# A bank copy on VectorE in the state-space stage, full-partition masks and later scaling and turns in the delta rule

## The chip, the cores and the metric

The program runs on one core of a Trainium2 chip. Its engines work side by side, each through its own instruction queue in order: TensorE (PE in the profile, with its weight loads as PEld), VectorE (DVE), ScalarE (ACT), GpSimd (POOL) and the queue of SyncE (SP), which only starts DMA transfers here. The metric is the device time of one execution in microseconds (us). A profile of one execution gives a row for each instruction.

## The reference, cut to what matters

Three layers on 256 tokens of width 1024: sparse attention, a state-space mixer and a gated delta rule, each followed by a gated feed-forward network. The change touches the second and the third mixer:

```python
def ssd_mixer(h, w_in, conv_w, conv_b, dt_bias, a_log, d_skip, norm_w, w_out):
    proj = h @ w_in
    z = proj[..., :SSD_D_INNER]
    xbc = jax.nn.silu(causal_dwconv(proj[..., SSD_D_INNER:SSD_D_INNER + SSD_CONV_DIM], conv_w, conv_b))
    ...
    y = ssd_scan(x_ssm, dt, a, bm, cm) + d_skip[:, None] * x_ssm
    y = y.reshape(b, s, SSD_D_INNER) * jax.nn.silu(z)
    ...

def gated_delta_rule(q, k, v, a, b, a_log, dt_bias):       # 8 heads, chunks of 64 tokens
    q = l2norm(q) * GDN_DK ** -0.5
    k = l2norm(k)
    ...
    kk = jnp.einsum("bhnid,bhnjd->bhnij", kc, kc)
    lower = jnp.where(strict, bc[..., :, None] * kk * decay, 0.0)
    rhs = jnp.concatenate([vc * bc[..., None], kc * (bc * jnp.exp(G))[..., None]], axis=-1)
    sol = lax.linalg.triangular_solve(lower + jnp.eye(CHUNK), rhs, left_side=True, lower=True, unit_diagonal=True)
    u, w = sol[..., :GDN_DV], sol[..., GDN_DV:]
    p = jnp.einsum("bhnid,bhnjd->bhnij", qc, kc) * decay
    qg = qc * jnp.exp(G)[..., None]
    ...                                                     # a scan over the 4 chunks with u, w, qg, kg, p
```

## The kernel before, in words

Everything is float32. A product x·w of a projection is made as three matmuls of rounded parts: ScalarE writes the upper part of a weight (`whi`, line 361), VectorE or GpSimd the rest (`wlo`, line 362), and TensorE adds whi·xhi, whi·xlo and wlo·xhi (line 308). A projection is cut into slabs of 256 output columns. A slab takes 48 matmuls of 128x256 into one PSUM bank of the tag `u`, of which there are two; a function `evac` then takes the bank away. Other small products use two banks of the tag `b`.

TensorE's order is that of the program text. The other engines' queues are put in order at build time by priority and by when an instruction is expected to be ready; VectorE, ScalarE and GpSimd then work them off strictly in that order. Slabs wait in a queue of generators; `pace()` puts as much of them between two steps of a chain as the next number of a table says (`GF` for the delta rule), `need(x)` runs the queue until x is done.

**State-space stage (ssd).** 20 of its slabs end in `convsilu` (12: B, C and x, a causal convolution of four taps, then x·sigmoid(x)) or `gate` (8: z). Since the row scale is already in the activations here, `scaled` (line 744) hands out the PSUM bank itself: `conv` (line 754) has ScalarE write the last tap into `u` and the last but one into `tap`, VectorE adds two more taps (line 767) and GpSimd the `tap` tile (line 769); `silu2` (line 771) follows. VectorE's taps and ScalarE's reads go to the bank.

**Delta rule (gdn).** Slabs k, then q, then v0 to v3 (the values of heads 0-1, 2-3, 4-5, 6-7), then z. The chain on VectorE: `L` (lower) is made; lines 1616 to 1622 turn its 16x16 diagonal blocks to the partitions by masks (`xp`, 8 instructions on 32 partitions each), a 32x32 transpose and a sum `yf`; 15 steps of a product and a sum (lines 1628 and 1629) invert all the blocks; lines 1691 to 1700 spread the inverse out again into `T` (in the buffer `et`, which the decay matrix for `Pt` held before) and `U`, each by a memset and 8 masked copies on 32 partitions. `T` and `U` then grow to 64x64 by two levels of products on TensorE (`lev16`, `lev32`), ending in `ub`. `nw` is `rw` times `ub` (32 matmuls), and `scan` runs over the chunks with `ub`, `bv`, `nw`, `kg`, `qn` and `Pt`.

Beside that chain: `scale(qn, rG)` (line 1585 on) multiplies the queries by exp(G): four times a `pace()`, two broadcast matmuls `b<-rh,sel` and one VectorE multiplication by that bank (line 1594), before `T` and `U` are made. `k_turn` (kt0 to kt3) transposes keys on TensorE and fills `kg` and `rw`. `v_turn(s)` (b0 to b3) transposes the finished value slab s (a tile named `gpsq`) on TensorE, and VectorE multiplies it into `bv` (line 1670). `POOL_PG` (line 1688) sends all rests of weights to GpSimd from that point of the text on.

## Time and profile before

| | us |
|---|---|
| median of 3 runs | 1330.9 |
| lowest and highest of them | 1323.39 and 1338.49 |
| the profiled execution, device time | 1329.81 |
| span of its trace | 1328.0 |
| granted TensorE clock, mean over the span | 0.964 |
| TensorE / VectorE / ScalarE / GpSimd busy | 1246.6 / 896.1 / 715.9 / 226.9 |

Times in the trace count from the start of the span; the device time is 1.8 us longer than the span. The state-space stage lies at about 412 to 622 us, the delta rule at about 875 to 1092 us. The granted clock is 1.00 at TensorE's full speed (2.4 GHz) and 0.50 at half. An idle time in square brackets stands before the instruction that it delayed, with what ended it.

### The profile page before, as it was taken

Reading aid. Unit: us, or ns where it says so; the run is one execution under the profiler, and the core shown is the slowest. Engines: PE = TensorE matmul, PEld = TensorE weight load, DVE = VectorE, ACT = ScalarE, POOL = GpSimd, SP = SyncE. Lnnn points to the kernel's source line nnn. Section 1 sums busy time; section 2 is a strip of 40 time slices with the busy share of each in tenths; the row PEclk is TensorE's granted clock in tenths of the full one; section 3 lists DMA queues with packets and bytes.
Section 4 is the critical chain, followed back from the end, with each engine's and each line's share of the span. In section 5 each row is a group of like instructions: output and inputs, shape, how many; then the busy total and the mean of one; then the engine's idle time right before and its main releaser. Section 6 shows DMA issues by size and latency. Waiting matters only on the chain.

```text
span 1328.0 us, 22701 instructions
## 1 busy us (share of the span) xinstructions
PE 1246.6 (94%) x8874; PEld 1110.1 (84%) x8874; DVE 896.1 (67%) x1647; ACT 715.9 (54%) x1340; POOL 226.9 (17%) x149
## 2 busy tenths in 40 slices
...
GB/s 316 283 143 1 33 118 201 197 184 188 183 153 140 118 110 143 137 102 140 167 194 191 181 181 187 116 155 96 112 48 49 64 64 159 172 192 180 185 184 41
DMA packets 54108, 192.78 MB, mean 145 GB/s; under 512 B 6128, under 2 KB 6768, under 8 KB 53616
## 3 DMA queue, kind: packets, MB, share of 16 engines
...
## 4 chain that ended last, share of the span: by engine, by line
PE 49%; DVE 9%; issue 7%; ACT 3%; POOL 2%; DMA 0%; POOLq 0%; DVEq 0%; ACTq 0%
PE u L308 29%; PE acc L308 16%; PE b L308 3%; DVE u L767 2%; DVE wlo L362 1%; ACT whi L361 1%; PE b L313 1%; POOL wlo L362 1%; POOL x L1267 0%; POOL rs L457 0%; DVE et L1698 0%; DVE rs L459 0%; POOL l2r L1585 0%; DMA raw<-in_gdn_up_dram 0%; ACT u L762 0%
## 5 line engine op out<-in xcount | busy, mean ns | idle before, releaser
L361 ACT ACTIVATE whi<-raw 128x1024 fp32r<-128x1024 f32 (+1 forms) x342 | 356.1, 1048 | 255.9 <-PE u L308 122.2
L308 PE MATMUL u<-xhi,whi 128*128 128x256 f32 x1600 | 467.0, 292 | 12.3 <-DVE xp L1628 5.5
L362 DVE TENSOR_TENSOR wlo<-raw,whi 128x1024 fp32r<-128x1024 f32 (+1 forms) x283 | 351.3, 1247 | 183.8 <-ACT whi L361 181.7
L308 PE MATMUL u<-xlo,whi 128*128 128x256 f32 x1600 | 458.7, 287 | 0.0
L308 PE MATMUL u<-xhi,wlo 128*128 128x256 f32 x1600 | 458.6, 287 | 0.0
L308 PEld LDWEIGHTS u<-xhi,whi 128*128 128x128 f32 x1600 | 313.2, 196 | 20.5 <-issue 15.4
L308 PEld LDWEIGHTS u<-xlo,whi 128*128 128x128 f32 x1600 | 313.3, 196 | 2.3
L308 PEld LDWEIGHTS u<-xhi,wlo 128*128 128x128 f32 x1600 | 312.8, 196 | 0.0
L362 POOL TENSOR_TENSOR wlo<-raw,whi 128x1024 fp32r<-128x1024 f32 x59 | 145.4, 2474 | 207.5 <-ACT whi L361 205.0
L308 PE MATMUL acc<-whi,yhi 128*128 128x512 f32 x376 | 150.9, 401 | 0.1
L308 PE MATMUL acc<-whi,ylo 128*128 128x512 f32 x376 | 149.8, 398 | 0.6 <-DVE ylo L362 0.6
L308 PE MATMUL acc<-wlo,yhi 128*128 128x512 f32 x376 | 149.8, 398 | 0.0
L574 POOL TENSOR_TENSOR post<-post,mhalf 128x1 f32<-128x1 f32 x12 | 6.5, 544 | 533.3 <-DVE post L573 523.2
L308 PEld LDWEIGHTS acc<-whi,ylo 128*128 128x128 f32 x376 | 71.1, 189 | 18.4 <-DVE ylo L362 1.0
L308 PEld LDWEIGHTS acc<-whi,yhi 128*128 128x128 f32 x376 | 71.4, 190 | 15.6 <-ACT yhi L361 0.6
L308 PEld LDWEIGHTS acc<-wlo,yhi 128*128 128x128 f32 x376 | 70.9, 189 | 14.3
L361 ACT ACTIVATE yhi<-y 128x256 fp32r<-128x256 f32 x66 | 27.2, 412 | 41.7 <-DVE y L851 41.6
L767 DVE SCALAR_TENSOR_TENSOR u<-u,par,u 128x254 f32<-128x254 f32 (+2 forms) x100 | 46.0, 473 | 5.1 <-ACT u L760 2.4
L535 DVE SCALAR_TENSOR_TENSOR xlo<-b,par,xhi 128x128 fp32r<-128x128 f32 x80 | 24.7, 345 | 29.8 <-ACT xhi L534 29.4
L767 DVE SCALAR_TENSOR_TENSOR uv<-p,par,uv 128x255 f32<-128x255 f32 x80 | 42.6, 532 | 0.1
L308 PE MATMUL acc<-whi,xhi 128*128 128x256 f32 x160 | 34.2, 295 | 8.9 <-ACT xhi L534 8.9
L534 ACT ACTIVATE xhi<-b,par 128x128 fp32r<-128x128 f32 x80 | 25.5, 366 | 31.5 <-PE b L313 28.4
...
## 6 DMA issues: line engine op xcount, KB each, us to landing
...
```

Source lines behind the costliest of these rows:

```text
L308: self.nc.tensor.matmul(out, lhsT, rhs, start=start, stop=stop, skip_group_check=True)
L313: self.nc.tensor.transpose(out, in_, self.c("ident", n)[:, :n])
L361: self.nc.scalar.activation(hi, src, AF.Copy)
L362: return (lo_engine or self.nc.vector).tensor_sub(lo, src, hi.bitcast(F32))
L534: act = nc.scalar.activation(h, ps, AF.Copy, scale=self.pc(gain, k))
L535: return act, nc.vector.scalar_tensor_tensor(l, ps, self.pc(gain, k), h.bitcast(F32), op0=ALU.mult, op1=ALU.subtract)
L574: nc.gpsimd.tensor_tensor(r[:, one], ms[:, one], self.mhalf, op=ALU.pow)
L767: nc.vector.scalar_tensor_tensor(u[c][:, sh:], p[c][:, :S - sh], col(c, taps - 1 - sh), u[c][:, sh:], op0=ALU.mult, op1=ALU.add)
```

## The change

- **State-space stage.** `scaled` gets an argument `copy`; with it, and no row scale, VectorE copies the whole bank (128x512) into an SBUF tile `p` first, at high priority, and everything after it reads `p`. The tanh of `silu2` is written over `p` (or over `u` for the gates) and not into a tile of its own. GpSimd's addition of `tap` now stands before VectorE's two taps.
- **Delta rule, masks.** Four masks `block16` on all 128 partitions take the place of the pairs on 32 partitions: `xp` takes 4 instructions, of which two also add, and `T` and `U` 4 each without a memset. The sign moves into the sum `yf`.
- **Delta rule, order.** `scale(qn, rG)` comes after `ub`, its four places in `GF` are 0.0, and its old share (2.5 + 5.3) is one number 7.8 at the pace before `lev16`. b2 and b3 come after `nw`, straight before the scan.

```diff
@@ -38,7 +38,7 @@
 NF = (1.8, 4.3, 1.0, 1.7, 0.0, 25.4, 27.1, 36.4, 3.6, 0.6, 0.0, 1.7, 0.6, 0.0, 5.9, 0.0, 17.5, 0.6, 1.4, 1.6, 2.0, 0.0, 0.3, 0.9, 22.3, 0.7, 3.9, 10.1, 17.8, 8.3, 2.0, 7.7, 15.3)
 ATT = 1
 BF = (1.7, 1.8, 0.0, 1.5, 1.5, 9.5, 1.5, 1.3, 0.0, 1.5, 2.5, 9.5, 1.5, 2.5, 0.0, 1.5, 1.5, 0.0)
-GF = (5.0, 5.3, 5.2, 9.6, 0.0, 2.5, 0.0, 0.0, 5.3, 0.9, 2.0, 0.3, 0.0, 9.0, 15.1, 28.2, 3.0, 6.1, 0.0, 0.0, 1.3, 0.2, 2.3, 0.9, 1.8, 0.0, 0.5, 0.9, 0.0, 1.3, 0.7, 1.3, 0.0, 0.0, 0.0, 4.0, 2.1, 1.2, 1.3, 0.0, 1.0, 0.0, 0.3, 1.2, 0.0, 0.0, 2.1, 9.5, 0.0, 19.3)
+GF = (5.0, 5.3, 5.2, 9.6, 7.8, 0.9, 2.0, 0.3, 0.0, 9.0, 0.0, 0.0, 0.0, 0.0, 15.1, 28.2, 3.0, 6.1, 0.0, 0.0, 1.3, 0.2, 2.3, 0.9, 1.8, 0.0, 0.5, 0.9, 0.0, 1.3, 0.7, 1.3, 0.0, 0.0, 0.0, 4.0, 2.1, 1.2, 1.3, 0.0, 1.0, 0.0, 0.3, 1.2, 0.0, 0.0, 2.1, 9.5, 0.0, 19.3)
 W_POOL = ()
 W_AHEAD = 62
 LEAD_N = 108
@@ -86,8 +86,8 @@
     put("sel32", (np.arange(64)[:, None] % 32 == np.arange(32)[None, :]))
     put("sel8", (np.arange(40)[:, None] % 32 == np.arange(8)[None, :]))
     put("half", np.stack([i < 64, i >= 64], 1))
-    put("neg16", -np.stack([i % 32 < 16, i % 32 >= 16], 1).astype(np.float32))
-    put("pos16", np.stack([i % 32 < 16, i % 32 >= 16], 1))
+    block = np.stack([(i % 64 // 32 == b) & (i % 32 // 16 == a) for b in range(2) for a in range(2)], 1).astype(np.float32)
+    put("block16", block)
     q = np.stack([i, i + 128], 1)
     ok = (np.arange(16)[None, None, :] * 16 + 31) <= q[:, :, None]
     put("cmask", ok.reshape(P, 32))
@@ -741,8 +741,13 @@
             self.need("tail")
         return x
 
-    def scaled(self, pool, ps, rb, tag="p", bufs=2):
-
+    def scaled(self, pool, ps, rb, tag="p", bufs=2, copy=False):
+
+        if rb is None and copy:
+            p = pool.tile([P, 2, S], F32, tag=tag, name=self.nm(tag), bufs=bufs)
+            with self.tc.high_priority(offset=URGENT // 2):
+                self.nc.vector.tensor_copy(p, ps.rearrange("p (c s) -> p c s", c=2))
+            return p
         if rb is None:
             return ps.rearrange("p (c s) -> p c s", c=2)
         p = pool.tile([P, 2, S], F32, tag=tag, name=self.nm(tag), bufs=bufs)
@@ -762,11 +767,11 @@
                 nc.scalar.activation(u[c], p[c], AF.Identity, scale=col(c, taps - 1), bias=self.pc(bias, i[c]))
             if pool is not None:
                 nc.scalar.activation(pool[c], p[c], AF.Copy, scale=col(c, taps - 2))
+            if pool is not None:
+                nc.gpsimd.tensor_add(u[c][:, 1:], u[c][:, 1:], pool[c][:, :S - 1])
         for c in both:
             for sh in range(1 if pool is None else 2, taps):
                 nc.vector.scalar_tensor_tensor(u[c][:, sh:], p[c][:, :S - sh], col(c, taps - 1 - sh), u[c][:, sh:], op0=ALU.mult, op1=ALU.add)
-            if pool is not None:
-                nc.gpsimd.tensor_add(u[c][:, 1:], u[c][:, 1:], pool[c][:, :S - 1])
 
     def silu2(self, out, u, th):
 
@@ -1149,18 +1154,18 @@
             def convsilu(key, i, b=1):
 
                 def evac(ps, x):
-                    p = self.scaled(sp, ps, x.rb)
+                    p = self.scaled(sp, ps, x.rb, copy=True)
                     u, o = t("u", [P, 2, S], b=2), t(key if b == 1 else key[0], [P, 2, S], b=b)
                     pool = [self.np_.tile([P, S], F32, tag="sq", name=self.nm("tap"), bufs=3) for _ in range(2)]
                     self.conv((u[:, 0], u[:, 1]), (p[:, 0], p[:, 1]), "scw", (i, i + 1), 4, "scb", pool)
-                    self.silu2(o, u, t("th", [P, 2, S], b=2))
+                    self.silu2(o, u, p)
                     out[key] = o
                 return evac
 
             def gate(key):
                 def evac(ps, x):
-                    u, o = self.scaled(sp, ps, x.rb), t("z", [P, 2, S], b=4)
-                    self.silu2(o, u, t("th", [P, 2, S], b=2))
+                    u, o = self.scaled(sp, ps, x.rb, copy=True), t("z", [P, 2, S], b=4)
+                    self.silu2(o, u, t("u", [P, 2, S], b=2))
                     out[key] = o
                 return evac
 
@@ -1613,13 +1618,16 @@
 
             xp, yt = t("xp", [P, 16, 32]), t("yt", [P, 16, 32])
             yf, tb = (spare(tag, 1).rearrange("p (a b) -> p a b", a=16) for tag in ("psum", "sqs"))
-            quads = [(slice(32 * q, 32 * q + 32), 32 * (q % 2)) for q in range(4)]
-            for qs, o in quads:
-                for a in range(2):
-                    nc.vector.tensor_scalar(xp[qs, :, 16 * a:16 * a + 16].rearrange("p j u -> p u j"),
-                                            L[qs, :, o + 16 * a:o + 16 * a + 16], self.c("neg16")[qs, a:a + 1], None, op0=ALU.mult)
+            blocks = [(b, a, 32 * b + 16 * a) for b in range(2) for a in range(2)]
+            for b, a, o in blocks:
+                x16 = xp[:, :, 16 * a:16 * a + 16].rearrange("p j u -> p u j")
+                mask = self.c("block16")[:, 2 * b + a:2 * b + a + 1]
+                if b == 0:
+                    nc.vector.tensor_scalar(x16, L[:, :, o:o + 16], mask, None, op0=ALU.mult)
+                else:
+                    nc.vector.scalar_tensor_tensor(x16, L[:, :, o:o + 16], mask, x16, op0=ALU.mult, op1=ALU.add)
             nc.vector.transpose(yt.rearrange("p a b -> p (a b)"), xp.rearrange("p a b -> p (a b)"))
-            nc.vector.tensor_add(yf, yt[:, :, :16], yt[:, :, 16:])
+            nc.vector.scalar_tensor_tensor(yf, yt[:, :, :16], -1.0, yt[:, :, 16:], op0=ALU.mult, op1=ALU.subtract)
             pr = t("xp", [P, 16, 32]).rearrange("p a b -> p (a b)")
             nc.vector.memset(tb, 0.0)
             nc.vector.memset(tb.rearrange("p a b -> p (a b)")[:, ::17], 1.0)
@@ -1674,7 +1682,7 @@
             for s in range(4):
                 self.add(f"v{s}", v_slab(s))
                 self.add(f"kt{s}", k_turn(s // 2, s % 2))
-                if s:
+                if s in (1, 2):
                     self.add(f"b{s - 1}", v_turn(s - 1))
             self.pace()
             rq, rq2 = t("rq", [P, 2, 8]), t("rq2", [P, 2, 8])
@@ -1684,7 +1692,6 @@
             pq = each(lambda u, tt, h, c: (kn[:, h, cs(tt, c)], qn[:, h, cs(tt, c)]))
             for tt in range(2):
                 nc.vector.tensor_tensor(half(Pt, tt), pq[tt], half(et, tt), op=ALU.mult)
-            scale(qn, rG)
             self.pool_lo = POOL_PG
             with self.tc.high_priority(offset=URGENT // 2):
                 T, U = m("et"), m("U")
@@ -1692,12 +1699,9 @@
                     d2, z = t("xp", [P, 16, 2, 16]), t("yt", [P, 16, 32])
                     nc.vector.tensor_copy(d2, view[:, :, None, :].to_broadcast([P, 16, 2, 16]))
                     nc.vector.transpose(z.rearrange("p a b -> p (a b)"), d2.rearrange("p a b c -> p (a b c)"))
-                    nc.vector.memset(dst, 0.0)
-                    for qs, o in quads:
-                        for a in range(2):
-                            nc.vector.tensor_scalar(dst[qs, :, o + 16 * a:o + 16 * a + 16],
-                                                    z[qs, :, 16 * a:16 * a + 16].rearrange("p c u -> p u c"),
-                                                    self.c("pos16")[qs, a:a + 1], None, op0=ALU.mult)
+                    for b, a, o in blocks:
+                        nc.vector.tensor_scalar(dst[:, :, o:o + 16], z[:, :, 16 * a:16 * a + 16].rearrange("p c u -> p u c"),
+                                                self.c("block16")[:, 2 * b + a:2 * b + a + 1], None, op0=ALU.mult)
 
             def z_slab(s):
                 def evac(ps, x):
@@ -1705,8 +1709,6 @@
                         zs.append(t("rw", [P, 8, S]))
                     self.silu2(two(zs[0], s), self.scaled(gp, ps, x.rb), t("th", [P, 2, S]))
                 return evac
-
-            self.add("b3", v_turn(3))
 
 
             self.pace()
@@ -1745,6 +1747,8 @@
                     nc.vector.tensor_tensor(half(ub, tt)[rs(c), :, rs(c)], half(U, tt)[rs(c)], pu[tt][rs(c)], op=ALU.subtract)
             self.pace()
 
+            scale(qn, rG)
+
 
             self.need("kt3")
             nw = t("kn", [P, 16, P])
@@ -1759,6 +1763,8 @@
                                          AF.Copy, scale=-1.0)
             self.gains(gp, "el")
             z = [up(12 + s, x, z_slab(s)) for s in range(4)]
+            self.add("b2", v_turn(2))
+            self.add("b3", v_turn(3))
             self.add("z1", chain(z[0], z[1]))
             self.add("z3", between(attention(), chain(z[2], z[3]), 3) if LATE else chain(z[2], z[3]))
             self.need("b3")
```

TensorE, from the second level's last products to the scan. `b<-cst,kn` is kt3, `b<-cst,gpsq` are b2 and b3, `b<-ad,rw` is `nw`, `b<-rh,sel` is the scaling of the queries, `acc<-bv,ad` the start of the scan. Before:

```order
L308 MATMUL acc_11275<-el_10239,et_10971 64x64 x16
L313 MATMUL b_11328<-cst,kn_9636 128x128 x4
L313 MATMUL b_11338<-cst,gpsq_11044 128x128 x4
L313 MATMUL b_11345<-cst,gpsq_11324 128x128 x4
L308 MATMUL b_11353<-ad_11308,rw_9639 128x128 x4
L308 MATMUL b_11359<-ad_11308,rw_9639 128x128 x4
L308 MATMUL b_11365<-ad_11308,rw_9639 128x128 x4
L308 MATMUL b_11371<-ad_11308,rw_9639 128x128 x4
L308 MATMUL acc_11380<-bv_10676,ad_11308 128x128 x2
```

TensorE at the same place now:

```order
L308 MATMUL acc_11273<-el_10267,et_10918 64x64 x16
L313 MATMUL b_11326<-cst,kn_9664 128x128 x4
L308 MATMUL b_11336<-rh_10496,sel_81 128x256 x2
L308 MATMUL b_11340<-rh_10496,sel_81 128x256 x2
L308 MATMUL b_11344<-rh_10496,sel_81 128x256 x2
L308 MATMUL b_11348<-rh_10496,sel_81 128x256 x2
L308 MATMUL b_11353<-ad_11306,rw_9667 128x128 x4
L308 MATMUL b_11359<-ad_11306,rw_9667 128x128 x4
L308 MATMUL b_11365<-ad_11306,rw_9667 128x128 x4
L308 MATMUL b_11371<-ad_11306,rw_9667 128x128 x4
L313 MATMUL b_11379<-cst,gpsq_11042 128x128 x4
L313 MATMUL b_11386<-cst,gpsq_11322 128x128 x4
```

The transposes of the last two value slabs went behind `nw`, and the eight broadcasts of the queries' scale, which stood among the slabs v1 and v2, came in ahead of it.

VectorE, from the second half of `Pt` on (`u<-u,par,u` are taps of slab v1, `et` and `U` the masked copies). Before:

```order
L1686 TENSOR_TENSOR Pt_10857<-acc_10859,et_10240 128x512
L1594 TENSOR_TENSOR qn_9637<-qn_9637,b_10894 128x512
L1695 MEMSET et_10971 128x1024
L1639 TENSOR_TENSOR kg_9638<-b_10917,egl_10134 128x512
L1698 TENSOR_SCALAR et_10971<-yt_10974,cst 32x16x16 x8
L767 SCALAR_TENSOR_TENSOR u_10904<-u_10773,par,u_10904 128x255
L1694 STREAM_TRANSPOSE yt_10987<-xp_10986 128x512
L767 SCALAR_TENSOR_TENSOR u_10904<-u_10773,par,u_10904 128x254
L1698 TENSOR_SCALAR U_10972<-yt_10987,cst 32x16x16 x8
L767 SCALAR_TENSOR_TENSOR u_10904<-u_10773,par,u_10904 128x253
L767 SCALAR_TENSOR_TENSOR u_10904<-u_10773,par,u_10904 128x255
L1594 TENSOR_TENSOR qn_9637<-qn_9637,b_10959 128x512
```

VectorE at the same place now:

```order
L1694 TENSOR_TENSOR Pt_10881<-acc_10883,et_10268 128x512
L1703 TENSOR_SCALAR et_10918<-yt_10921,cst 128x16x16 x4
L1647 TENSOR_TENSOR kg_9666<-b_10955,egl_10162 128x512
L1701 STREAM_TRANSPOSE yt_10929<-xp_10928 128x512
L774 SCALAR_TENSOR_TENSOR u_10942<-u_10797,par,u_10942 128x255
L1703 TENSOR_SCALAR U_10919<-yt_10929,cst 128x16x16 x4
L774 SCALAR_TENSOR_TENSOR u_10942<-u_10797,par,u_10942 128x254
L1678 TENSOR_TENSOR bv_10700<-b_10965,bhr_10442 128x256
L774 SCALAR_TENSOR_TENSOR u_10942<-u_10797,par,u_10942 128x253
L774 SCALAR_TENSOR_TENSOR u_10942<-u_10797,par,u_10942 128x255
L1678 TENSOR_TENSOR bv_10700<-b_10965,bhr_10442 128x256
L774 SCALAR_TENSOR_TENSOR u_10942<-u_10797,par,u_10942 128x254
```

The multiplications of `qn` and the memset are gone from here, and 8 masked copies are 4.

VectorE in the state-space stage, about the two last slabs before its scan (`x` is the result of a slab, `ah` the row sums that the first broadcast there needs). Before:

```order
L362 TENSOR_TENSOR wlo_5273<-raw_5270,whi_5272 128x1024
L1198 TENSOR_TENSOR boff_5019<-acs_5018 128x32
L1199 TENSOR_SCALAR nacs_5020<-acs_5018 128x32
L774 SCALAR_TENSOR_TENSOR x_4949<-th_4962,u_4948 128x512
L767 SCALAR_TENSOR_TENSOR u_5036<-u_4977,par,u_5036 128x254
L1206 TENSOR_TENSOR ah_5056<-b_5053,ah_5056 32x256
L767 SCALAR_TENSOR_TENSOR u_5036<-u_4977,par,u_5036 128x253
```

VectorE at the same place now:

```order
L362 TENSOR_TENSOR wlo_5281<-raw_5278,whi_5280 128x1024
L1203 TENSOR_TENSOR boff_5024<-acs_5023 128x32
L1204 TENSOR_SCALAR nacs_5025<-acs_5023 128x32
L749 COPY p_5041<-u_4982 128x512
L779 SCALAR_TENSOR_TENSOR x_4955<-p_4952,u_4954 128x512
L1211 TENSOR_TENSOR ah_5062<-b_5059,ah_5062 32x256
L1221 SCALAR_TENSOR_TENSOR cb_5069<-b_5066,cst 128x128
L774 SCALAR_TENSOR_TENSOR u_5043<-p_5041,par,u_5043 128x254
```

The copy of the bank came in, the taps moved behind `ah`, and a tap's first operand is `p` in SBUF in place of the PSUM bank.

## Rows read from the trace of the kernel before

**Rows 1.** The page: busy time, share of the span and instructions of each engine.
```profile
PE 1246.6 (94%) x8874; PEld 1110.1 (84%) x8874; DVE 896.1 (67%) x1647; ACT 715.9 (54%) x1340; POOL 226.9 (17%) x149
```

**Rows 2.** Windows over both stages: length, busy us (instructions) by engine, granted clock.
```profile
412.00:622.00 210.00, 192.23 (x1324) 171.20 (x1325) 150.02 (x245) 113.70 (x230) 63.07 (x46) 0.94 0.38 126
875.00:1092.00 217.00, 183.59 (x1687) 173.67 (x1686) 124.90 (x270) 87.52 (x191) 58.41 (x25) 0.87 0.23 78
```

**Rows 3.** Waits of TensorE, 400 to 660 us: in total, times, longest.
```profile
PE b L308 <- DVE ah L1206: 2.8, 1, 2.8
...
PE u L308 <- DVE u L767: 1.6, 1, 1.6
```

**Rows 4.** Waits of TensorE, 860 to 1120 us.
```profile
PE b L308 <- DVE qn L1594: 9.1, 1, 9.1
PE b L313 <- DVE gpsq L774: 7.6, 1, 7.6
PE u L308 <- DVE xp L1628: 5.5, 1, 5.5
```

**Rows 5.** Timeline of TensorE in the delta rule: start, duration, instruction.
```profile
973.90 0.79 PE L308 MATMUL b<-rh,sel 40*128 40x256 f32 x2 [9.09 <-DVE qn L1594]
...
984.32 1.85 PE L308 MATMUL acc<-U,ad 64*64 64x64 f32 x56
...
999.98 0.66 PE L313 MATMUL b<-cst,kn 128*128 128x128 f32 x4
...
1008.65 1.11 PE L313 MATMUL b<-cst,gpsq 128*128 128x128 f32 x4 [7.58 <-DVE gpsq L774]
1009.56 4.85 PE L308 MATMUL b<-ad,rw 128*128 128x128 f32 x32
1014.24 1.95 PE L308 MATMUL acc<-bv,ad 128*128 128x128 f32 x16
```

**Rows 6.** Timeline of VectorE in the delta rule.
```profile
915.35 2.96 DVE L1619 TENSOR_SCALAR xp<-ad,cst 32x256 f32<-32x256 f32 x8
...
959.59 1.28 DVE L1686 TENSOR_TENSOR Pt<-acc,et 128x512 f32<-128x512 f32 x2
...
961.62 0.91 DVE L1695 MEMSET et<- 128x1024 f32 x1 [0.16 <-DVE qn L1594]
...
963.00 4.79 DVE L1698 TENSOR_SCALAR et<-yt,cst 32x256 f32<-32x256 f32 x8
...
969.21 3.16 DVE L1698 TENSOR_SCALAR U<-yt,cst 32x256 f32<-32x256 f32 x8
...
973.16 0.68 DVE L1594 TENSOR_TENSOR qn<-qn,b 128x512 f32<-128x512 f32 x1
...
975.80 0.69 DVE L774 SCALAR_TENSOR_TENSOR gpsq<-th,u 128x512 f32<-128x512 f32 x1
...
1001.04 2.78 DVE L1745 TENSOR_TENSOR ad<-U,acc 64x512 f32<-64x512 f32 x4
```

**Rows 7.** The window behind TensorE's longest wait: columns as in rows 2.
```profile
974.00:981.00 7.00, 6.35 (x27) 5.83 (x28) 3.35 (x8) 0.63 (x1) 0.00 (x0) 0.50 0.00 0
```

**Rows 8.** Groups of VectorE by form: busy us, mean ns of one, idle before.
```profile
L1085 DVE COPY pt<-b 128x512 f32<-128x512 f32 x12 | 8.2, 686 | 3.0 <-PE u L308 2.3 <-PE b L313 0.6
```

**Rows 9.** Timeline of VectorE and GpSimd while GpSimd writes a `wlo`.
```profile
663.33 2.41 POOL L362 TENSOR_TENSOR wlo<-raw,whi 128x1024 fp32r<-128x1024 f32 x1 [4.39 <-ACT whi L361]
663.36 2.67 DVE L767 SCALAR_TENSOR_TENSOR uv<-p,par,uv 128x255 f32<-128x255 f32 x1
...
456.49 2.40 POOL L362 TENSOR_TENSOR wlo<-raw,whi 128x1024 fp32r<-128x1024 f32 x1 [5.09 <-ACT whi L361]
457.10 0.86 DVE L767 SCALAR_TENSOR_TENSOR u<-u,par,u 128x253 f32<-128x253 f32 x2
```

**Rows 10.** Groups of GpSimd by form, 405 to 625 us.
```profile
L362 POOL TENSOR_TENSOR wlo<-raw,whi 128x1024 fp32r<-128x1024 f32 x15 | 37.6, 2516 | 42.1 <-ACT whi L361 42.1
L769 POOL TENSOR_TENSOR u<-u,tap 128x255 f32<-128x255 f32 x24 | 19.6, 820 | 44.6 <-DVE u L767 32.2 <-ACT ee L1248 9.9 <-DVE spw L783 1.1
```

## The prediction

> **What bounds the kernel now.** I read the page first: TensorE is busy for 1246.6 us, 94% of the span, and no other engine for more than two thirds of it apart from the weight loads [rows 1]. TensorE's order is fixed by the text, so a change elsewhere can win only where TensorE waits, or runs at the lower clock after it waited. The second view is the windows over the two stages that are touched [rows 2]: in the state-space stage TensorE is busy for 192.2 of 210 us at a granted clock of 0.94, in the delta rule for 183.6 of 217 us at 0.87. The third is the list of its waits in each. In the state-space stage the waits that belong to this change are small: 1.6 us once for a bank of a slab that VectorE's taps still read, and 2.8 us for `ah`, which stands in VectorE's queue behind a tap [rows 3]. In the delta rule three single waits make up 22 us [rows 4]: 9.1 for a multiplication of the queries, 7.6 for the finished slab v3, and 5.5 for a bank behind the chain. The fourth view, the timelines, says what VectorE does meanwhile [rows 5, 6]. The second `qn` runs only at 973.16, behind all 16 masked copies into `et` and `U`. The 7 us behind that wait run at a clock of 0.50 [rows 7], which is 1.2 GHz.
>
> **The masks of `xp`.** Eight instructions took 2.96 us, 0.37 each, and each covers 256 elements in a partition [rows 6]. The new ones have the same 256 elements on four times the partitions, and there are four of them. Two multiply at 0.37; two also add, for which a tap of 253 elements (0.43 each in a pair [rows 9]) is the nearest row, so about 0.45. The sum is 1.65, and 1.3 us are gone. They lie in the chain that ends TensorE's 5.5 us wait [rows 4], so I take all of it: **-1.3**. The ends are 0, if the tap that frees the bank waits for something else, and -1.5, if all four cost 0.37.
>
> **From `Pt` to `lev16`.** Before, TensorE needed 24.7 us from the end of the products for `Pt` (when VectorE starts `Pt`, 959.59) to `lev16` (984.32) [rows 5, 6]. Out of that go the 9.1 us wait, half of the 6.35 busy us at the lower clock (3.2 [rows 7]), and the four pairs of broadcasts, 0.79 a pair at half speed [rows 5] and so 0.4 at full (with a little latency about 2). That leaves 10.4 us of slabs and turns, and TensorE would be at `lev16` at about 970, and at b1 (the turn of v1), which stands a turn and six matmuls ahead of it, some 1.4 us earlier, at 968.6.
>
> Now b1 needs v1 finished, and that is the new last wait. VectorE finished v1 at 976.5 (975.80 + 0.69), 16.9 us after 959.59 [rows 6]. From this I take out three `qn` of 0.6, the memset of 0.9, half of the 4.79 us of masks for `et` and half of the 3.16 us for `U`: 6.7 us. One `kg` (0.6) comes in ahead, as VectorE's order shows. So v1 is done at 959.59 + 16.9 - 6.7 + 0.6 = 970.4. But TensorE is faster here, and GpSimd has two more `wlo` in this stretch, which hold VectorE up (the 4.79 against 3.16 us of the same eight masks shows 1.6 us for one); I allow 0 to 3.2 and take 1.6: 972. TensorE then waits for some 3.4 us, and `lev16` starts at 973.4: 10.9 us earlier. A wait of that length was followed by half speed before [rows 7], for up to 7 us, which costs up to 3.4; I take 2. **-8.9**, with ends at -13 (no hold-up, no loss of clock) and -5 (two hold-ups and the whole loss).
>
> Between `lev16` and kt3 the order stays, 15.7 us [rows 5], and VectorE's queue there holds the same work as before.
>
> **From kt3 to the scan.** Before: 14.3 us from 999.98 to 1014.24, with 7.6 of wait for v3 and `nw` in 4.85 [rows 5]. Now the broadcasts of the queries' scale stand where b2 and b3 stood. They use the two `b` banks, each is freed by one `qn` of 0.68, and VectorE is busy with `ub` until 3.8 us after kt3's start (1001.04 + 2.78 [rows 6]). By VectorE's new order a tap, `qn`, two taps, `kg`, a tap, `qn`, a tap, `qn`, v3's end and the last `qn` follow, about 6.5 us with a wait of 0.7 for the tanh. The third `qn` frees the first bank for `nw` at about 8.5 to 9 us, `nw` takes four rounds of 1.0 to 1.2 us (4.85 before), the second held until the last `qn` at 10.3, and b2 and b3 another 1.2: the scan starts 14.3 to 15.2 us after kt3. So the 7.6 us wait isn't removed; four waits of 2 us on banks take its place: **0**. The ends are -4, if VectorE has v3's taps behind it by then, and +3.
>
> **The copies of the banks.** There are 20, and a copy of 128x512 from PSUM takes 0.69 us [rows 8]: 13.7 us more for VectorE in a stage where it is busy for 150 of 210 us [rows 2]. The 60 idle us cover that; without this cover it would be 13.7 us on the path. The 1.6 us wait for a bank goes, since the bank is free one copy after its last matmul; what can be late next is the copy itself, behind older work in VectorE's queue, and I count 1.2 of the 1.6. The 2.8 us for `ah` may shrink, since the order now has `ah` ahead of the taps, but a copy ahead of it; I count nothing. **-1.2**, with ends at -4.4 (both waits) and the third rival below. The memset of `U` lay off the path, and tanh over `p` or `u` is the same work in another tile.
>
> **The sum.** Against the profiled 1329.8 us (1328.0 of span and 1.8 around it, 1.1 below the median of 1330.9): 1329.8 - 1.3 - 8.9 - 0 - 1.2 = **1318.4**, 12.5 us or 0.9% below the median. The new kernel and this one can be told apart from about 1%, here 13 us.
>
> **Rivals.** *Both waits of the delta rule vanish.* If v1 is there when TensorE turns it, and the four `qn` keep up, then 9.1, 7.6 and 1.3 us go, and with them the 3.2 us that were lost at half speed behind the first wait. With 1.6 for the bank that is 22.8, so **1307.0**. For it speaks that VectorE is freed of 6.7 us; against it that its remaining work up to the end of v1 is 10.8 us long where TensorE is at b1 after 9.
>
> *The waits only move.* If GpSimd's two more `wlo` hold VectorE twice, the half clock follows in full and the bank waits after kt3 are 3 us longer: -1.3 - 5 + 3 + 0 gives **1326.5**. For it speaks that VectorE is the engine that ends all three waits.
>
> *The taps are locked out in the state-space stage, and it is slower than before.* Before, the taps read PSUM, and two of them ran in 0.86 us while GpSimd wrote a `wlo`; in the next stage a tap that reads SBUF took 2.67 us, as long as GpSimd's `wlo` of 2.41 beside it [rows 9]. The change makes all 48 taps of the stage of the second kind, and puts GpSimd's 24 additions (0.82 us each [rows 10]) right ahead of them, with 15 `wlo` of 2.5. If each addition holds a tap, VectorE loses 20 us, at most 57 with the `wlo`. With the copies that is 34 to 71 us against 60 idle. VectorE's idle time isn't evenly spread, so I take it that held time beyond the 20 us of the additions comes onto the path; at 45 us held, 25 do, and the sum is 1329.8 - 1.3 - 8.9 + 25 = **1344.6**. Against it: the operations with two SBUF operands in this stage run with GpSimd already, and TensorE waits little. The Trainium skill ("SBUF — State Buffer", "Who interferes with whom") states this lock: a VectorE instruction with two SBUF inputs contends with a GpSimd instruction that reads SBUF, and the second one blocks fully. By that rule the copies turn free taps into ones that can be blocked, which is this rival; the 2.67 us tap agrees.
>
> **How the numbers follow.** The forecast, 1318.4 with its own range 1311 to 1325, gets 0.48; the vanishing waits 0.20; the moved waits 0.22; the lock-out 0.10. A gain of over 1% ends at 1317.6: a little under half of the forecast's share (0.22), and the first rival (0.20), make 0.43 with a trace of the others; slower by over 1% needs more than 1344.2, half of the lock-out, 0.05; 0.52 remain. The range reaches down to the four best ends together (1329.8 - 1.5 - 13 - 4 - 4.4 = 1306.9) less 4 us, about half of the distance between the fastest run and the median of before, which leaves out a third of the first rival (0.07); above it takes in the moved waits with their ends (1329.8 - 0 - 5 + 3 + 0, and again 4 to 6 us for the runs) and leaves out the lock-out (0.10): 1303 to 1334.
>
> **What would show it.** In the new profile: no 9.1 us wait of TensorE for `qn` before `lev16`, but one of 3 to 6 us for `gpsq` at b1; `lev16` 9 to 12 us earlier; several waits for `qn` of 1 to 4 us between kt3 and `nw`, and none of 7.6 for v3; four masks of about 0.37 to 0.45 us; 20 copies of 0.69; VectorE's busy time in the state-space stage up by 14 to 30 us and TensorE's waits there within 3 us of before. It is wrong if the taps' mean there passes 0.8 us and TensorE's waits on VectorE grow with it, or if b1 doesn't wait at all.

## The result: 0.5% slower, and the profile after

The changed kernel takes 1333.3 us (median of 20 executions, 1329.8 to 1346.0); the kernel before 1331.2 in the same comparison. The ratio is 1.0051, with a 95% interval of 1.0028 to 1.0075: slower by half a per cent where 0.9% faster was forecast. The quotient of the two medians is only 1.0016 and that of the means 1.0031 (without one execution of 1738.0 us of the kernel before), so the loss is clear of noise and its size is not. The profiled execution took 1329.9 us, 1328.1 of span.

The windows over the two touched stages (length, then busy us of TensorE, its weight loads, VectorE, ScalarE, GpSimd; granted clock), to be laid beside [rows 2]:

```profile
412.00:622.00 210.00, 187.88 (x1300) 167.32 (x1301) 159.44 (x255) 114.39 (x226) 67.37 (x46) 0.92 0.35 116
875.00:1092.00 217.00, 188.08 (x1738) 177.82 (x1738) 127.47 (x269) 91.37 (x200) 67.64 (x29) 0.90 0.25 84
```

TensorE as a whole is as busy as in [rows 1] (1246.4 us), and VectorE has 12.3 us more:

```profile
PE 1246.4 (94%) x8874; PEld 1109.9 (84%) x8874; DVE 908.4 (68%) x1651; ACT 718.9 (54%) x1340; POOL 236.5 (18%) x151
```

Of the windows' rows: TensorE is busy for 4.4 us less in the state-space window, so it does less of its work there; in the delta rule it is busy for 4.5 us more. The gain and the loss lie where these two rows say. TensorE's waits from 400 to 660 us (total, times, longest; `x`, `w` and `ah` are tiles that VectorE makes in this stage):

```profile
PE acc L313 <- ACT tail L681: 7.7, 1, 7.7
...
PE b L308 <- DVE x L1266: 3.3, 3, 1.9
...
PE b L308 <- DVE w L1256: 3.0, 2, 2.3
...
PE b L308 <- DVE ah L1211: 1.4, 1, 1.4
```

Beside [rows 3]: the 1.6 us wait for a bank is gone and `ah` fell from 2.8 to 1.4, but a wait of 7.7 us stands at the stage's entry, for `tail` (the last columns of the projection, which ScalarE takes out of PSUM). Before, it was this row of the same view:

```profile
PE acc L313 <- ACT tail L681: 1.9, 1, 1.9
```

The entry in the timelines of the changed kernel (start, duration, instruction, idle time before it):

```profile
402.74 11.36 POOL L362 TENSOR_TENSOR wlo<-raw,whi 128x1024 fp32r<-128x1024 f32 x4 [15.87 <-ACT whi L361]
...
406.99 4.90 DVE L362 TENSOR_TENSOR wlo<-raw,whi 128x1024 fp32r<-128x1024 f32 x2 [0.59 <-ACT whi L361]
411.81 1.27 DVE L749 COPY p<-acc 128x512 f32<-128x512 f32 x2
414.81 3.61 DVE L774 SCALAR_TENSOR_TENSOR u<-p,par,u 128x254 f32<-128x254 f32 x6 [1.72 <-POOL u L771]
...
412.53 0.60 ACT L767 ACTIVATE u<-p,par 128x256 f32<-128x256 f32 x1 [2.40 <-DVE p L749]
...
417.60 0.63 ACT L778 ACTIVATE p<-u 128x512 f32<-128x512 f32 x1 [1.81 <-DVE u L774]
...
418.54 0.36 ACT L681 ACTIVATE tail<-acc 32x256 f32<-32x256 f32 x1
```

Before, ScalarE read the bank itself, and `tail` came right behind four such reads:

```profile
410.54 0.55 ACT L762 ACTIVATE u<-acc,par 128x256 f32<-128x256 f32 x1
...
413.40 0.36 ACT L681 ACTIVATE tail<-acc 32x256 f32<-32x256 f32 x1
```

Read the changed kernel's rows as a chain: VectorE's two `wlo` end at 411.8, only then comes the copy, so ScalarE waits 2.4 us for it; GpSimd's additions stand behind four `wlo` (to 414.1) and now ahead of VectorE's taps, so these wait 1.7; the tanh waits for the taps, and `tail` stands behind the tanh.

In the delta rule, TensorE's waits from 860 to 1120 us, against [rows 4]:

```profile
PE u L308 <- DVE u L774: 6.2, 3, 5.8
PE b L313 <- DVE gpsq L779: 5.4, 1, 5.4
PE u L308 <- DVE xp L1636: 4.8, 1, 4.8
PE b L308 <- DVE qn L1599: 4.3, 2, 3.9
...
PE b L308 <- ACT rw L1650: 1.8, 1, 1.8
```

The 9.1 and the 7.6 us are gone, the waits at b1 (5.4) and for `qn` are the ones forecast, and one of 5.8 us for a bank of a slab is new. The same stretch of TensorE's timeline, against [rows 5]:

```profile
951.08 0.55 PE L308 MATMUL u<-xhi,whi 128*128 128x256 f32 x1 [5.82 <-DVE u L774]
...
979.37 1.08 PE L313 MATMUL b<-cst,gpsq 128*128 128x128 f32 x4 [5.42 <-DVE gpsq L779]
...
981.67 3.13 PE L308 MATMUL acc<-U,ad 64*64 64x64 f32 x64
...
998.36 0.66 PE L313 MATMUL b<-cst,kn 128*128 128x128 f32 x4
...
1003.36 0.80 PE L308 MATMUL b<-rh,sel 40*128 40x256 f32 x2 [3.92 <-DVE qn L1599]
...
1014.36 1.84 PE L308 MATMUL acc<-bv,ad 128*128 128x128 f32 x15
```

### The profile page after: what moved, and what is told of

Read it like the earlier page. It is cut to its first block, busy times and chain, and to the rows that moved or that the text cites. A ratio compares the mean times of both kernels' runs of the same rounds, so it can differ in the third digit from the quotient of the medians.

```text
span 1328.1 us, 22708 instructions
## 1 busy us (share of the span) xinstructions
PE 1246.4 (94%) x8874; PEld 1109.9 (84%) x8874; DVE 908.4 (68%) x1651; ACT 718.9 (54%) x1340; POOL 236.5 (18%) x151
## 4 chain that ended last, share of the span: by engine, by line
PE 47%; DVE 11%; issue 6%; ACT 3%; POOL 2%; POOLq 0%; DVEq 0%; ACTq 0%
PE u L308 26%; PE acc L308 17%; PE b L308 3%; DVE u L774 2%; DVE wlo L362 2%; ACT whi L361 1%; PE b L313 1%; DVE xp L1636 1%; POOL u L771 0%; DVE p L749 0%; POOL wlo L362 0%; ACT xhi L534 0%; POOL rs L457 0%; DVE rs L459 0%; POOL l2r L1590 0%
## 5 line engine op out<-in xcount | busy, mean ns | idle before, releaser
L308 PE MATMUL u<-xhi,whi 128*128 128x256 f32 x1600 | 466.9, 292 | 14.7 <-DVE u L774 6.2
L362 DVE TENSOR_TENSOR wlo<-raw,whi 128x1024 fp32r<-128x1024 f32 (+1 forms) x281 | 343.8, 1229 | 177.3 <-ACT whi L361 173.7
L362 POOL TENSOR_TENSOR wlo<-raw,whi 128x1024 fp32r<-128x1024 f32 x61 | 153.9, 2532 | 203.2 <-ACT whi L361 200.7
L1051 ACT ACTIVATE p<-acc,mx,r 128x128 f32<-128x128 f32 (+1 forms) x64 | 32.0, 510 | 18.8 <-DVE mx L1048 17.0
```

Of the source, the lines that this page charges most:

```text
L308: self.nc.tensor.matmul(out, lhsT, rhs, start=start, stop=stop, skip_group_check=True)
L362: return (lo_engine or self.nc.vector).tensor_sub(lo, src, hi.bitcast(F32))
L1051: nc.scalar.activation(p[:, b, :], s3[:, b, :], AF.Exp, scale=r8[:, qt:qt + 1], bias=mx[:, b:b + 1], accum_out=den[:, b:b + 1])
```

## The experiments

Three numbers are used throughout. From the timeline of each profile: the **stage stretch**, from the start of the last matmul of `tail` to the last broadcast of `rs` in the state-space stage, with TensorE's idle time in it. **Half speed**: the granted clock c of an execution is a mean of two levels (1.00 and 0.50), so TensorE stood at the lower one for 2(1-c) of the span. Half of this time is taken as its price. That is a high estimate: in the changed kernel's trace the 128x256 matmuls of a slab start every 0.120 us (median) at the higher level and every 0.213 us at the lower, which makes the price 0.44 of the time, and over the executions of the kernel before the time rises by 0.40 us for each us at half speed. **Without clock** is a time less that price. The table has medians over the executions of each kernel. The kernel before has 130 of them, from five comparisons, whose own medians of the last column go from 1279.7 to 1281.9 us; so 1 to 2 us between two rows of that column say nothing.

| kernel | ratio to before (95%) | median us | half speed us | without clock us |
|---|---|---|---|---|
| before | 1 | 1329.1 | 95.6 | 1281.0 |
| after | 1.0051 (1.0028 to 1.0075) | 1333.3 | 101.0 | 1282.1 |
| s_only | 1.0074 (1.0040 to 1.0108) | 1338.6 | 106.9 | 1284.9 |
| g_only | 0.9947 (0.9908 to 0.9986) | 1322.6 | 85.9 | 1278.9 |
| tail_first | 1.0022 (0.9989 to 1.0055) | 1331.7 | 98.5 | 1283.3 |
| add_behind | 1.0028 (0.9989 to 1.0068) | 1333.5 | 103.8 | 1281.3 |
| copy18 | 1.0020 (0.9991 to 1.0048) | 1331.3 | 100.9 | 1281.5 |
| add_only | 0.9996 (0.9961 to 1.0031) | 1329.1 | 92.9 | 1282.5 |
| act_copy | 1.0015 (0.9980 to 1.0049) | 1327.7 | 96.8 | 1280.6 |
| act_behind | 0.9984 (0.9954 to 1.0014) | 1329.3 | 93.0 | 1282.4 |
| tap_psum | 1.0018 (0.9995 to 1.0040) | 1330.4 | 96.9 | 1281.5 |
| dead_copy | 1.0008 (0.9967 to 1.0048) | 1328.6 | 91.5 | 1282.8 |
| gate_free | 1.0027 (0.9996 to 1.0059) | 1330.3 | 99.6 | 1279.8 |
| g_wlo | 0.9958 (0.9925 to 0.9991) | 1322.4 | 93.7 | 1275.1 |
| m_timed | 0.9949 (0.9914 to 0.9984) | 1322.2 | 88.5 | 1277.5 |
| m_turns | 0.9951 (0.9914 to 0.9988) | 1323.3 | 96.5 | 1275.4 |
| nw_first | 0.9887 (0.9861 to 0.9912) | 1314.7 | 82.7 | 1274.1 |

### The two halves of the change: g_only and s_only

g_only is the changed kernel with the state-space stage as before; s_only the reverse. (Of each edit the lines that say it best are shown; three points stand for the rest.)

```diff
-                    p = self.scaled(sp, ps, x.rb, copy=True)
+                    p = self.scaled(sp, ps, x.rb)
...
```

> The delta rule's part alone (masks, order), the state-space stage as before. Theory A (the state-space stage loses what the delta rule gains): the delta rule's windows are as in the changed kernel, 7 us shorter than before from the wait for spp to 1116 us, and the state-space stage's waits are those of before, so 7 us below the kernel before, a ratio of 0.995 (0.992 to 0.997). Rival B (the delta rule gains nothing lasting, since the new 5.8 us wait for a bank of the slabs takes the gain): a ratio of 0.999 to 1.002.

> The state-space stage's part alone (copies, tanh in the copy's tile, GpSimd's additions ahead of the taps), the delta rule as before. Theory A: TensorE's wait for tail at the start of the stage is 7.7 us as in the changed kernel (1.9 before), the stage's end comes 5.5 to 8 us later, and the time is 6 to 8 us above the kernel before, a ratio of 1.004 to 1.007. Rival B: the stage costs nothing, 0.999 to 1.002.

Theory A held in both, with 0.9947 and 1.0074; the second is a little above the end of what was said (1.007). By these ratios the delta rule's part gains 7 us and the state-space stage's part loses 10, each give or take some 5. s_only shows the same 7.7 us for `tail`, and the stage stretch takes 210.4 us; g_only shows the same 5.8 us for a bank.

### Is the loss at the stage's entry? tail_first, copy18

tail_first puts ScalarE's write of `tail` ahead:

```diff
-            nc.scalar.activation(flat, ps[:n, :S], AF.Copy)
+            with self.tc.high_priority(offset=URGENT):
+                nc.scalar.activation(flat, ps[:n, :S], AF.Copy)
```

> The changed kernel, with ScalarE's write of tail in the state-space and later stages at urgent priority: it stands right behind the first ScalarE read of the copy, not behind seven more and a tanh. Theory A (the loss is the stage's entry: the copy waits for two wlo on VectorE, ScalarE for the copy, the taps for GpSimd's additions behind four wlo, and tail for all of them): TensorE's wait for tail falls from 7.7 to about 2.5 us, the ssd stage ends 5 us earlier, and the time is 5 to 6 us below the changed kernel, ratio to the kernel before 0.999 to 1.002. Rival C (VectorE's taps are held by GpSimd all along the stage, and the loss is there): the wait for tail falls, but waits for x, w and ah take its place, and the time stays within 2 us of the changed kernel.

The wait for `tail` fell as theory A said. The ratio, 1.0022, stands just above what A said, and its interval reaches up to the changed kernel's 1.0051, so the time decides little. The profile decides: TensorE's waits in the stage are now

```profile
PE b L308 <- DVE ah L1212: 5.1, 1, 5.1
...
PE acc L313 <- ACT tail L682: 2.6, 1, 2.6
```

Of the 5.1 us that `tail` lost, `ah` took 3.7 (1.4 to 5.1), and later waits the rest: the row of the longest wait had named a place, not the cause. The stretch took 212.2 us, with 23.2 idle, where the changed kernel has 210.6 and 22.8. copy18 leaves the first two slabs uncopied:

```diff
-                    p = self.scaled(sp, ps, x.rb, copy=True)
+                    c = bool(x.hi)
+                    p = self.scaled(sp, ps, x.rb, copy=c)
...
```

> The changed kernel, but the first two slabs (B and C, which end in banks of the tag acc at the stage's entry) are not copied; the other 18 are. Theory A (the loss sits at the stage's entry, where the copy waits for VectorE's two wlo and ScalarE for the copy): TensorE's wait for tail is about 2.5 us in place of 7.7 and its wait for ah stays under 4, its idle time between the tail matmuls and the stage's last rs broadcast falls from 22.8 to about 18 us (17.9 in the kernel before), and the time is 4 to 7 us below the changed kernel, a ratio to the kernel before of 0.998 to 1.002. Rival C (VectorE is too full in the whole stage, since taps wait for GpSimd's additions and read SBUF): the idle time stays above 21 us, in waits for ah, x and w, and the ratio is 1.003 to 1.006.

Rival C was right on the waits: `tail` 4.3, `ah` 3.6, 22.9 us idle, 212.1 us. The ratio (1.0020) is at the upper end of what theory A said and below rival C's. By the idle time, the entry alone as the cause fell.

### Copies or additions: add_behind, add_only

add_behind moves GpSimd's additions back behind the taps and keeps the copies; add_only is the kernel before with only the additions ahead.

```diff
+            if pool is not None:
+                nc.gpsimd.tensor_add(u[c][:, 1:], u[c][:, 1:], pool[c][:, :S - 1])
         for c in both:
...
```

> The changed kernel, with GpSimd's additions behind VectorE's taps as before (the copies stay). Theory A: the taps at the stage's entry don't wait 1.7 us for GpSimd, so the wait for tail is about 6 us in place of 7.7, and the time 1 to 3 us below the changed kernel. Rival C (the lock of VectorE's taps): VectorE's 9.5 us of idle time before taps go, the taps' mean falls from 0.65 to about 0.5 us, and the time falls by 4 to 7 us.

> The kernel before, with only GpSimd's additions moved ahead of VectorE's taps (no copies). Theory A: TensorE's wait for tail is 2 to 2.5 us, VectorE's taps read PSUM and keep their 0.47 us, and the time is within 0.3% of the kernel before. Rival C: VectorE waits 9 us for GpSimd's additions as in the changed kernel, TensorE's idle time in the stage rises by 3 us or more from 17.9, and the ratio is 1.002 to 1.005.

The additions alone cost nothing (0.9996, idle 18.7), though they too raise the waits for `tail` and `ah` to 4.3 and 4.2; later ones shrink by nearly as much. The copies without the additions ahead cost: 22.0 us idle in a stretch of 207.9. The wait for `tail` is 7.2 us there, where theory A said about 6. For VectorE's taps rival C's picture holds, as the groups of the changed kernel show (busy us, mean ns, idle before and who ended it):

```profile
L774 DVE SCALAR_TENSOR_TENSOR u<-p,par,u 128x254 f32<-128x254 f32 x24 | 15.5, 654 | 9.6 <-POOL u L771 9.5
...
L774 DVE SCALAR_TENSOR_TENSOR u<-p,par,u 128x253 f32<-128x253 f32 x24 | 12.4, 523 | 0.4
```

Before, out of the banks `u`, they waited 1.9 us in all and took 0.47 each:

```profile
L767 DVE SCALAR_TENSOR_TENSOR u<-u,par,u 128x253 f32<-128x253 f32 x20 | 9.5, 474 | 0.3
L767 DVE SCALAR_TENSOR_TENSOR u<-u,par,u 128x254 f32<-128x254 f32 x20 | 9.5, 473 | 1.9 <-ACT tap L764 1.9
```

The copies took what [rows 8] said:

```profile
L749 DVE COPY p<-u 128x512 f32<-128x512 f32 x18 | 12.3, 684 | 0.6 <-PE u L308 0.6
```

Without the additions ahead the taps don't become free: in add_behind they took 0.68 and 0.55, where rival C had said about 0.5.

### Load or link: act_copy, act_behind, tap_psum, dead_copy, gate_free

A copy per slab can cost as work in VectorE's queue, as a step between a slab and its readers, or because taps out of SBUF are held by GpSimd. act_copy lets ScalarE copy:

```diff
-                self.nc.vector.tensor_copy(p, ps.rearrange("p (c s) -> p c s", c=2))
+                self.nc.scalar.activation(p, ps.rearrange("p (c s) -> p c s", c=2), AF.Copy)
```

> The changed kernel, with the 20 copies of the banks made by ScalarE in place of VectorE (same place in the text, same priority). Theory F (VectorE's queue sets the pace of the stage up to its first statistics, and nine copies of 0.68 us there lengthen it): from the last tail matmul to the first statistics (the first matmuls of sq) TensorE takes 66 to 69 us, as in the kernel before (66.7) and not 72.6 as in the changed one; the time is 4 to 7 us below the changed kernel, a ratio to the kernel before of 0.994 to 0.999. Rival A (the copy is a link between slab and ScalarE's reads, whoever makes it, and the additions of GpSimd ahead of the taps do the rest): that stretch takes 71 us or more, and the ratio is 1.001 to 1.005.

The front of the stage, from the last matmul of `tail` to the first statistics (the first matmuls of `sq`), took 69.2 us, just outside what theory F said, and the ratio is as rival A said. act_behind is act_copy with the additions behind the taps:

> The changed kernel with the copies made by ScalarE and GpSimd's additions behind the taps as before; only the copy itself and taps out of SBUF are left of the state-space stage's part. If the additions' place costs with copies what separates 69.2 us (copies by ScalarE) from 66.7 (before) up to the first statistics, that stretch is 66 to 68 us here and the stage's is 199 to 203; if the copy as a link between slab and ScalarE's reads is the cost, they stay at 69 or more and 204 or more.

70.5 and 207.9: by the profile it isn't the additions. (Besides the copy and the taps out of SBUF, the tanh in the copy's tile is left here too.) The ratio, 0.9984, is the lowest of the kernels with copies, below the changed kernel's interval and still above g_only's 0.9947; without clock nothing of that is left (1282.4 against 1282.1). The taps were held most here:

```profile
L772 DVE SCALAR_TENSOR_TENSOR u<-p,par,u 128x254 f32<-128x254 f32 x24 | 18.9, 792 | 0.2
...
L772 DVE SCALAR_TENSOR_TENSOR u<-p,par,u 128x253 f32<-128x253 f32 x24 | 14.2, 596 | 0.4
```

tap_psum gives the taps their PSUM operand back and keeps the copies (`src` is the bank):

```diff
-                nc.vector.scalar_tensor_tensor(u[c][:, sh:], p[c][:, :S - sh], col(c, taps - 1 - sh), u[c][:, sh:], op0=ALU.mult, op1=ALU.add)
+                nc.vector.scalar_tensor_tensor(u[c][:, sh:], (src or p)[c][:, :S - sh], col(c, taps - 1 - sh), u[c][:, sh:], op0=ALU.mult, op1=ALU.add)
...
```

> The changed kernel, but VectorE's two taps read the PSUM bank again; ScalarE reads the copy, and all 20 copies stay. Theory L (the taps out of SBUF are held by GpSimd, and that is the larger part of what the copies cost): the taps' mean falls from 0.65 and 0.52 to 0.47 us, from the last tail matmul to the first statistics TensorE takes 68 to 70 us in place of 72.6, and from it to the stage's last rs broadcast 204 us or less in place of 210.6. Theory F (it is the copies' own 0.68 us in VectorE's queue, and the wait of ScalarE and of the taps behind them): the taps' mean falls, but the two stretches stay above 71 and 207 us.

Split: the taps were free again at 0.475 us and the front took 66.4 us, even less than theory L said, but the stage stretch 208.1, as theory F said. The banks are now held by the taps, behind the copies:

```profile
PE u L308 <- DVE u L774: 6.4, 3, 4.3
```

dead_copy keeps VectorE's copies, and everything reads the bank:

```diff
-                    p = self.scaled(sp, ps, x.rb, copy=True)
+                    q, p = self.scaled(sp, ps, x.rb, copy=True), ps.rearrange("p (c s) -> p c s", c=2)
...
```

> The changed kernel, all 20 copies on VectorE as before, but nothing reads them: ScalarE, the taps and the last multiplication read the PSUM bank; the copy's tile only takes the tanh. VectorE has the copies' 0.68 us each, but the copy is no link between a slab and its readers. Theory M (the link costs: what is computed from a slab comes a copy later, and TensorE waits for it in the front of the stage, whoever makes the copy): TensorE's idle time from the last tail matmul to the last rs broadcast falls from 22.8 to 17 to 19.5 us, and the stretch without what half speed adds from 196.9 to 192 to 195 us. Theory F (VectorE's load): idle stays above 21.5 and the stretch at 196 us or more.

Theory M fell, and F's numbers came: 22.3 us idle, 209.1 us with 12.1 of half speed, so 197.0. Here too the banks are waited for (5.6 us). gate_free drops the 8 gate copies:

> The changed kernel without the copies of the 8 gate slabs; the 12 of the convolutions stay. Theory M: the gates' results are needed late (behind the scan), so their copies cost little, and what is lost is lost at the convolutions: idle 21 to 23 us, the stretch without what half speed adds 196 us or more, the ratio within 0.2% of the changed kernel's 1.005. Theory F: 5.5 us of 13.7 leave VectorE's queue, and the idle time falls by 2 us or more.

As theory M said of the gates: 21.9 us idle and 196.1 without half speed, though a ratio of 1.0027, a little under its bounds; nearly all of the loss is made by the 12 copies of the convolutions. Laid side by side (stage stretch in us; "adds" is half of TensorE's busy time inside the half-speed stretches):

| kernels | stretch | idle | half speed adds | rest |
|---|---|---|---|---|
| 8 profiles with the stage as before | 198.0 to 204.3 | 16.7 to 19.1 | 3.3 to 13.4 | 190.9 to 194.7 |
| add_only | 201.3 | 18.7 | 7.9 | 193.4 |
| after / s_only | 210.6 / 210.4 | 22.8 / 22.7 | 13.7 / 13.6 | 196.9 / 196.7 |
| tail_first / copy18 | 212.2 / 212.1 | 23.2 / 22.9 | 14.7 / 14.9 | 197.5 / 197.2 |
| add_behind / gate_free | 207.9 / 208.5 | 22.0 / 21.9 | 11.4 / 12.5 | 196.5 / 196.1 |
| act_copy / act_behind | 204.6 / 207.9 | 21.9 / 23.5 | 7.9 / 9.8 | 196.7 / 198.1 |
| tap_psum / dead_copy | 208.1 / 209.1 | 23.1 / 22.3 | 10.2 / 12.1 | 197.9 / 197.0 |

The eight profiles without any part of the change there are idle for 18.0 us in the mean, 16.7 to 19.1; every kernel that copies the convolutions' slabs is idle for 21.9 to 23.5, some 4 to 5.5 us more than that mean, on whichever engine and whatever reads the copy. Only the wait that shows it changes (`tail`, `ah`, `x`, `w`, or the bank). That is shown. The many executions agree, as far as they reach: all nine kernels that have both parts of the change stand above g_only without clock, by 0.9 to 4.4 us. How the half speed in the stretch comes out is not shown by one profile each: it adds 3.3 to 13.4 us with the stage as before.

Parted at the first statistics, the traces say more. TensorE's idle time in us:

| kernels | front | rest of the stretch |
|---|---|---|
| 8 profiles with the stage as before | 7.9 to 10.3 | 8.8 |
| add_only | 10.1 | 8.7 |
| copies, taps read the copy (8 kernels) | 12.2 to 13.5 | 8.8 to 10.1 |
| tap_psum / dead_copy (copies, taps read the bank) | 10.1 / 9.6 | 13.0 / 12.7 |

The changed kernel and tap_psum differ in the taps' first operand alone. So what the change loses in the front goes with the taps reading the copy; with the bank as their operand, that loss is gone, and one more wait for a bank behind the front (4.3 us, 4.1 in dead_copy) takes its place. What stays open is how much of the front's loss is the taps' longer time beside GpSimd and how much their wait for the copy. All ten kernels with copies also write the tanh over the copy's tile; no run takes that apart, but in tap_psum it is there and the front's loss isn't.

### The delta rule: m_only, m_timed, m_scale, m_turns, g_wlo, nw_first

m_only and m_timed are one kernel, the masks alone on the kernel before:

```diff
-                    nc.vector.memset(dst, 0.0)
-                    for qs, o in quads:
+                    for b, a, o in blocks:
...
```

> The kernel before, with only the masks changed. TensorE's wait for xp falls by about 1 us (5.5 to 4.5), its 9.1 us wait for qn before lev16 falls to 5 to 7 us since four masks into et and four into U and no memset cost VectorE 3 us less, and its wait for a bank of the slabs there stays at 1.3 us, since no wlo has changed its engine. From the products for Pt to lev16 25 us (28.3 before, 19.3 in the changed kernel). Rival: the masks alone bring most of the gain there, 20 us.

> The masks alone on the kernel before, again, now timed. Theory G (the masks carry the delta rule's gain; what the new order saves before lev16 it gives back in new waits for a bank of the slabs, for v1 and for qn): a ratio of 0.991 to 0.996, no worse than masks and order together (0.9947). Rival H (the single fast run of the masks was luck of the clock): 0.997 to 1.000.

The masks alone (1316.1 us in a single execution, then 0.9949) give what masks and order give together (0.9947): theory G. In m_only the 9.1 us wait for `qn` fell to 1.7, where 5 to 7 were expected, and the bank wait before `Pt` vanished (1.3 to nothing), where it was expected to stay.

m_scale adds to the masks only the later scaling, m_turns only the later turns (shown):

```diff
-                if s:
+                if s in (1, 2):
                     self.add(f"b{s - 1}", v_turn(s - 1))
...
```

> The masks, and of the new order only the later scaling of the queries (behind ub); the turns of v2 and v3 stay in their old places. Theory G: TensorE's 5.8 us wait for a bank of the slabs is there (it comes with the scaling's place, which moves two wlo to GpSimd), from the products for Pt to lev16 18 to 20 us, and from kt3 to the scan 17 to 19 us, since both the 7.6 us wait for v3 and the waits for banks of qn stand ahead of the scan; no faster than the masks alone from the wait for xp to the scan (87.5 us). Rival: it is 2 us or more faster there.

> The masks, and of the new order only the later turns of v2 and v3 (behind nw); the scaling of the queries stays in its old place. With the queries' banks not in between, nw starts when rw is there, some 6 us after kt3, and runs while VectorE finishes v3: from kt3 to the scan 12 to 13 us in place of 15.4 with the masks alone and 16.0 in the changed kernel; 2 to 3 us below the masks alone, a ratio of 0.989 to 0.995. Rival: v3 stays the last wait, since its turn stands behind nw and needs a bank, and the stretch stays at 14 us or more, the ratio within 0.1% of the masks alone.

TensorE's stretches in us, one profile each; a is from the end of the wait for `xp` to the products for `Pt`, b to `lev16`, c to kt3, d to the scan:

| kernel | a | b | c | d | sum |
|---|---|---|---|---|---|
| before | 32.7 | 28.3 | 15.7 | 14.3 | 91.0 |
| after | 37.4 | 19.3 | 16.7 | 16.0 | 89.4 |
| m_timed (masks) | 32.6 | 23.7 | 15.7 | 15.5 | 87.5 |
| m_scale (masks, scaling) | 37.1 | 19.2 | 16.7 | 18.3 | 91.3 |
| m_turns (masks, turns) | 32.6 | 23.9 | 15.7 | 10.2 | 82.3 |
| g_wlo | 32.6 | 19.7 | 17.3 | 16.4 | 86.0 |
| nw_first | 32.6 | 19.7 | 17.3 | 13.8 | 83.4 |

As theory G said, the later scaling is no gain: it saves 4.5 us in b and gives 4.4 back in a, 1.0 in c and 2.8 in d (m_scale has one execution, 1325.4 us). The later turns save 5.3 in d, more than expected, since `nw` runs while v3 is finished. In m_turns' timeline of TensorE `nw` starts 2.5 us after kt3, and the two turns follow it without the 7.6 us:

```profile
1002.13 0.66 PE L313 MATMUL b<-cst,kn 128*128 128x128 f32 x4
1004.62 1.16 PE L308 MATMUL b<-ad,rw 128*128 128x128 f32 x8 [1.84 <-DVE ad L1744]
...
1011.82 0.66 PE L313 MATMUL b<-cst,gpsq 128*128 128x128 f32 x4 [0.24 <-ACT kn L1757]
```

Yet m_turns is no faster than the masks alone (0.9951). Without clock it is 2.1 us better; in the median it stood 8 us longer at half speed (96.5 against 88.5), for which the table takes 4. Its single executions stood there for 73 to 109 us and those of m_timed for 63 to 101, so these 8 us are not clear of noise.

g_wlo takes g_only and gives two `wlo` back to VectorE:

```diff
+            self.fill(2.5)
             self.pool_lo = POOL_PG
...
```

> The delta rule's part alone, and the two wlo that it had moved from VectorE to GpSimd are VectorE's again (the switch to GpSimd stands 2.5 us of slab work later, TensorE's order unchanged). Theory D (TensorE's new 5.8 us wait for a bank of the slabs comes from the four wlo that GpSimd writes beside the last steps of the inversion, which held three products of VectorE for 2.6, 1.6 and 1.6 us): these products take 0.4 to 0.6 us, the wait falls to 2.5 us or less, the products for Pt come 3 to 5 us earlier, and the time is 2 to 5 us below the delta rule's part alone, a ratio to the kernel before of 0.991 to 0.994. Rival E (VectorE has no room there in any case: two wlo of 1.2 us more on it take the place of the hold-ups): the wait stays above 4 us, and the ratio at 0.994 to 0.997.

Theory D's mechanism is shown. In the changed kernel three products of the inversion ran beside GpSimd's `wlo` (timelines of VectorE and GpSimd):

```profile
941.23 2.62 DVE L1636 TENSOR_TENSOR xp<-gsqs,gpsum 128x144 f32<-128x144 f32 x1
945.62 1.63 DVE L1636 TENSOR_TENSOR xp<-gsqs,gpsum 128x196 f32<-128x196 f32 x1
948.23 1.64 DVE L1636 TENSOR_TENSOR xp<-gsqs,gpsum 128x225 f32<-128x225 f32 x1
...
938.36 5.21 POOL L362 TENSOR_TENSOR wlo<-raw,whi 128x1024 fp32r<-128x1024 f32 x2 [23.87 <-ACT whi L361]
944.49 4.97 POOL L362 TENSOR_TENSOR wlo<-raw,whi 128x1024 fp32r<-128x1024 f32 x2 [0.92 <-ACT whi L361]
```

In g_wlo the same products are free, and TensorE's 5.8 us wait is gone:

```profile
935.71 0.41 DVE L1636 TENSOR_TENSOR xp<-gsqs,gpsum 128x144 f32<-128x144 f32 x1
...
939.16 0.50 DVE L1636 TENSOR_TENSOR xp<-gsqs,gpsum 128x196 f32<-128x196 f32 x1
940.62 0.55 DVE L1636 TENSOR_TENSOR xp<-gsqs,gpsum 128x225 f32<-128x225 f32 x1
```

Stretch a is 4.8 us shorter than in the changed kernel, as theory D said (3 to 5). The time, though, didn't move (0.9958): 3.8 us better without clock, 7.8 us more at half speed, which again lies within the scatter (76 to 117 us against 63 to 109 in g_only). nw_first adds to g_wlo that the scaling stands behind `nw` as well:

```diff
-            scale(qn, rG)
-
             self.need("kt3")
...
                                          AF.Copy, scale=-1.0)
+            scale(qn, rG)
```

> State-space stage as before; masks; the two wlo back on VectorE; turns of v2 and v3 and the scaling of the queries all behind nw. Expected from what the single runs gave: from the products for Pt to lev16 17 to 18 us (as with the scaling late), from kt3 to the scan 12 to 13.5 us (10.2 with the turns alone, and four broadcasts with their waits for qn), no wait of 5.8 us for a bank of the slabs; 2 to 4 us less than any of the single versions without the clock, a ratio to the kernel before of 0.990 to 0.994. Rival K (the clock takes it back: what TensorE waits less, it runs more at 1.2 GHz later): the stretches are as said, the half-speed stretches of the execution are longer than the 88 us of the masks alone, and the ratio stays at 0.994 to 0.996.

0.9887: 1.1% below the kernel before and, by the two ratios, 1.6% below the changed one; the fastest of all, in six executions. Its stretch d is 0.3 us above what was said, and b, with 19.7, is 1.7 above. Rival K didn't come, since half speed took less here (82.7 us). Without clock it is only 1.0 us below g_wlo and 1.3 below m_turns, where 2 to 4 were expected: the larger part of its lead over them is time at half speed, and no run shows whether the order brought that.

## Why the prediction was wrong

**What bounds the kernel.** TensorE's waits were the right place to look, and VectorE ended most of them. To call the state-space stage's waits small was the mistake behind the next point.

**The copies: the step that failed.** "The 60 idle us cover that" priced them at -1.2. The 1.6 us bank wait did go and `ah` fell by 1.4, but the stage stretch grew by 7.9 us (202.7 to 210.6), with 5.0 us more idle time and 3.5 more by half speed, and s_only is 0.74% slower. Of these 5.0 us, 4.0 lie in the front (9.1 to 13.1). A sum of idle time over a stage says nothing of when it is idle: in the stage's front TensorE waits for what is made from each slab, and there the copy and the taps that read it come too late. What was said to be late next, the copy itself behind older work in VectorE's queue, is what the entry shows.

**The third rival** had the place and half of the mechanism, at a chance of 0.10. Taps out of SBUF took longer: 0.65 and 0.52 us against 0.47, and 0.79 and 0.60 in act_behind. Giving them PSUM back (tap_psum) gave the front back, but not the stage, since waits for banks came in behind it. So the taps' operand goes with where TensorE waits, and taking it back alone doesn't save the time. Of the rule of the Trainium skill that stood beside it ("SBUF — State Buffer", "Who interferes with whom", an instruction with two SBUF inputs can be locked out by GpSimd) these rows and the 2.62 us product in the delta rule are agreeing cases; by it alone the whole loss would have gone with the taps' operand, and only the front's did. The Trainium skill also has, for element-wise work on a matmul's output, either to read PSUM or to copy to SBUF first if many operations follow ("VectorE: DVE Perf Modes", "Rules for kernel authors"). The copy brought nothing here: a tap that nothing held took about the same time out of SBUF (four in 1.66 us in add_behind) as out of PSUM (two in 0.86 [rows 9]).

**The masks of `xp`: -1.3**, measured -1.0 on VectorE (2.96 us from the first to the last before, 1.93 now): two multiply at 0.37, but the two that add took 0.69 each, not 0.45. TensorE's wait fell by 0.7. The masks of `U` are 0.39 each; those of `et` ran beside a `wlo`:

```profile
918.26 0.74 DVE L1626 TENSOR_SCALAR xp<-ad,cst 128x256 f32<-128x256 f32 x2
918.82 1.37 DVE L1628 SCALAR_TENSOR_TENSOR xp<-ad,cst,xp 128x256 f32<-128x256 f32 x2
...
967.29 3.78 DVE L1703 TENSOR_SCALAR et<-yt,cst 128x256 f32<-128x256 f32 x4
...
972.58 1.56 DVE L1703 TENSOR_SCALAR U<-yt,cst 128x256 f32<-128x256 f32 x4
```

**From `Pt` to `lev16`: -8.9**, measured -8.0, with the mechanism right: from VectorE's start of `Pt` (965.98) to `lev16` 15.7 us against 24.7, so 9.0 less, with the new wait at b1 where it was put (5.4 us, forecast 3.4), and 1.0 us given back behind it, where the window (as [rows 7]) still shows half speed:

```profile
977.00:984.00 7.00, 4.63 (x54) 4.43 (x56) 5.18 (x10) 2.68 (x8) 1.68 (x1) 0.51 0.46 152
```

**A term that was missing.** The two more `wlo` of GpSimd were looked for behind `Pt`; weights are prepared ahead, so they ran before it, beside the last steps of the inversion, and made the 5.8 us wait. Stretch a grew by 4.6 us. By the same token the scaling's new place was no gain: its price lay mostly in front of the stretch that was counted.

**From kt3 to the scan: 0**, measured +1.7 (14.3 to 16.0), inside the ends; the waits are 3.9, 1.8, 0.4 and 0.2 and not four of 2.

**The first two rivals.** The waits didn't vanish, b1 and the banks waited; nor did they only move: with -7 us the delta rule lies between the forecast's -10.2 and that rival's -3.3.

**The sum.** Where -12.5 us were forecast, the delta rule gave -7 and the state-space stage took +10 (g_only, s_only). What would have shown it wrong was named as taps over 0.8 us or no wait at b1; neither came. VectorE's busy time in the stage's window rose by 9.4 us and not by 14 to 30. The sign to name was a wait for anything made from a slab.
